# Thirty-two unused floats between the work tiles and the tiles of high parts, in a two-layer mLSTM and retention trunk

## The chip, the cores and the metric

The kernel runs on one core of one Trainium2 chip. The metric is the device time of one execution in microseconds. A core has a matrix engine (PE), three engines for elementwise work (VectorE or DVE, ScalarE or ACT, GpSimd or POOL), a queue engine that issues most transfers (SyncE or SP), and an on-chip memory, SBUF, of 128 partitions. A tile takes the same stretch of bytes in every partition, and that stretch starts at one address. The whole case is about those addresses.

## What is computed

Each of two layers takes x (1024 positions by 1024 features, float32) through

    h = RMSNorm(x) * (1 + scale) + shift          # scale, shift, gate from a conditioning vector
    p = h @ W_in                                  # queries, keys, values, gates for 8 heads of 256
    y_m = sigmoid(o) * LN(mLSTM(conv(q), conv(k), v)) * silu(z)   # heads 0 to 3, chunkwise
    y_r = LN(retention(rot(q), rot(k), v)) * silu(z)              # heads 4 to 7, chunkwise
    x = x + gate * (concat(y_m, y_r) @ W_out)

and a last RMSNorm follows. Nearly all arithmetic is in the two projections, W_in (1024 by 9224) and W_out (2048 by 1024).

## The kernel before

**Split products.** Float32 factors are split in two: a high part, rounded to the matrix engine's float32r, and a low part, the rest. `mm3` (L176 to L179) makes one product of three matmuls: high by high (L177), high by low (L178), low by high (L179). The first argument is the one held in the array (the weights of that matmul, loaded anew for each of the three); the second is streamed past it.

**Where the split tiles live.** The forms of h, the split outputs of the heads and the split keys of the state update lie in the pool `big`, whose 59 tiles of 512 floats are called `b`. A weight block arrives by a transfer in a tile `R`. `high` (L402) copies it on ACT to a tile `wH`, and `low` (L407 to L410) subtracts on DVE or POOL and writes the low part to another `R` tile. So a split weight block is one `wH` and one `R`. In the attention, `q` and `kc` hold high and low part of a chunk's queries and keys in one tile each; `cH`, `cL` hold the split state, `sH`, `sL` the split scores, `ring0` and `ring1` the values.

**Which tile is streamed and which is held.** In the paired products for q, k, z and o (`pair_product`, L758), in the first layer's output projection (`out_units`, L1278) and in the first blocks of a layer, the forms `b` are streamed (512 columns) and `wH`, `R` are held. In the products for v (`vpair_product`, L793; 256 columns) and in the last layer's output projection (512 columns) it is the other way round: `wH`, `R`, `wH` are streamed and `b` is held. The scores stream `q` past `kc` (`diagonal`, L1037, and `mm3`).

**Order.** The order of PE's instructions is the one written. The other engines' order is made by a planner that simulates the program, with priorities and a few places where the written order is kept. A generator clock (`launch`, `tick`) decides when side work is written.

**Addresses.** Three pools lie one after the other in SBUF: `cst`, `big`, `wrk`. In `wrk`, a tag's slots lie together, and tags follow in the order of their first use: `rows`, `R` (12 slots), `wgr`, `q` (2), `acc` (12), `wH` (5), then `sm1`, `cH`, `cL`, `COL`, `kc` and the small tiles, `dm`, `nd`, `sH`, `sL`, `cf`, `zt`. Slots are rounded up to 32 bytes. `b`, `R` and `q` have slots that are whole multiples of 256 bytes, so all of them start at one remainder modulo 256: 64. A slot of `acc` has 516 floats, 2064 bytes, rounded up to 2080. Twelve of them make 24960 bytes, which is 97 times 256 and 128 more. So everything after `acc` lies 128 bytes off: `wH` starts at remainder 192. In `cH` and `cL` the remainders are 0 and 32, in `kc` 64, in `sH` and `sL` 128, in `ring0` and `ring1` 64 and 96.

Of the kernel before, what the change touches and what calls it, by code (L numbers as in the profile page):

```python
# [11 lines left out]
F32 = mybir.dt.float32  # L12
# [7 lines left out]
P = 128  # L20
# [67 lines left out]
def tile_hybrid_trunk(ctx, tc, x, xt, c, positions, w_ada, b_ada, norm_g, w_in, w_blk, w_val, conv_w, conv_b,  # L88
# [9 lines left out]
    wrk = ctx.enter_context(tc.tile_pool(name="wrk", bufs=2))  # L98
# [6 lines left out]
    def nm(s):  # L105
        uid[0] += 1
        return f"{s}_{uid[0]}"

    def bt(dt=F32, n=512):
        return big.tile([P, n], dt, tag="b", name=nm("b"))  # L110

    def wt(tag, n, bufs, dt=F32):
        t = wrk.tile([P, 516 if tag == "acc" else n], dt, tag=tag, bufs=bufs, name=nm(tag))
        return t[:, 0:n] if tag == "acc" else t

    def ps_a():
# [101 lines left out]
    def load_ada_rows(l):  # L218
        rows = wt("rows", P, 2)
        Q.dma_start(rows[0:8, :], norm_g[l].rearrange("(r c) -> r c", c=P))  # L220
        Q.dma_start(rows[8:32, :], b_ada[l].rearrange("(r c) -> r c", c=P))
        return rows

    def load_head_rows(l):
        rows = wt("rows", P, 2)
        Q.dma_start(rows[0:16, :], conv_b[l].rearrange("(r c) -> r c", c=P))
        Q.dma_start(rows[16:80, :], conv_w[l].rearrange("t (r c) -> (t r) c", c=P))
        Q.dma_start(rows[80:88, :], gn_m[l].rearrange("(r c) -> r c", c=P))
        Q.dma_start(rows[88:96, :], gn_r[l].rearrange("(r c) -> r c", c=P))
        bg = cst.tile([P, 1], F32, tag=f"bg{l}", name=f"bg{l}")  # L230
        Q.dma_start(bg[0:4, :], b_fgate[l].unsqueeze(1))
        Q.dma_start(bg[32:36, :], b_igate[l].unsqueeze(1))
        return rows, bg
# [37 lines left out]
    def finish_gsh(l, k, n, psh, psc):  # L271
        cl = cols[l][0]
        V.tensor_tensor(gsh[l][:, 1, k:k + n], psh, cl[:, 104 + k:104 + k + n], ALU.add)
        t1 = wt("sm1", 4, 2)[:, 0:n]
        V.scalar_tensor_tensor(t1, psc, 1.0, cl[:, 112 + k:112 + k + n], ALU.add, ALU.add)
        V.tensor_tensor(gsh[l][:, 0, k:k + n], t1, cl[:, k:k + n], ALU.mult)
# [1194 lines left out]
    for l in range(DEPTH):  # L1471
# [23 lines left out]
        if l == 0:  # L1495
# [10 lines left out]
            for step in script.split():  # L1506
# [4 lines left out]
                if what in "SQ":  # L1511
                    half, tt, cc = arg
                    o, xi, acc = wt("acc", 512, NACC), xts[half][tt][cc], xss[half][:, tt, cc:cc + 1]
# [208 lines left out]
```

## Time and profile before

| | |
|---|---|
| median of three runs | 2225.32 us (2223.43 to 2238.9) |
| the profiled execution | 2226.27 us, of which the span of its instructions 2224.6 us |
| PE, matmuls | 2137.0 us busy, 96% of the span |
| PE, weight loads (beside the matmuls) | 1820.5 us, 82% |
| DVE | 1776.2 us, 80% |
| ACT | 1146.9 us, 52% |
| POOL | 945.0 us, 42% |

A matmul row's duration runs from its start to a modelled end, and matmuls overlap: the next one starts well before the end of the last. So rows of equal shape are compared with one another, and the rate of a stretch is read from the starts in the order of time. In a row such as `px<-b,wH` the first name after the arrow is the streamed tile and the second the held one.

### The profile page before, as it was taken

How to read it: one execution, taken by the hardware profiler on the slowest of the kernel's cores; microseconds unless marked ns; L12 is line 12 of the kernel's file. 1: busy time of each engine (PE TensorE's matmuls, PEld its weight loads, DVE VectorE, ACT ScalarE, POOL GpSimd, SP SyncE). 2: the span in 40 equal slices, each digit the busy share in tenths (PEclk: the TensorE clock that was granted, in tenths of full speed). 3: DMA queues.
4: the chain of work that ended last, by engine and by line, in shares of the span. 5: the costliest groups of instructions: out<-in, count | busy, mean ns of one | idle time of the engine just before them, and what ended most of it. 6: DMA issues, size and time to landing. Idle time of an engine off the chain costs nothing.

```text
span 2224.6 us, 35050 instructions
## 1 busy us (share of the span) xinstructions
PE 2137.0 (96%) x11489; PEld 1820.5 (82%) x11489; DVE 1776.2 (80%) x3139; ACT 1146.9 (52%) x2151; POOL 945.0 (42%) x820
## 2 busy tenths in 40 slices
PE   6899999999999999999999999999999899999998
PEld 5688888878988878888778788888988887888887
DVE  6898897989989988874639697888897798978563
ACT  7545335445556655653544434454555565655442
POOL 1443244444454454424466334444544444352313
PEclk9999999999999999999999999999999999999999
DMA  8268678787787767686632866877877676677874
GB/s 287 60 186 229 196 216 255 211 237 211 214 240 180 202 178 208 192 269 221 208 107 68 250 190 191 230 200 206 234 194 191 177 217 197 171 199 250 222 250 118
DMA packets 452836, 448.44 MB, mean 202 GB/s; under 512 B 191314, under 2 KB 310042, under 8 KB 452652
## 3 DMA queue, kind: packets, MB, share of 16 engines
q1 hardware_dynamic: 432924, 410.27, 59.8%
q0 software_dynamic: 19584, 35.66, 10.7%
q8 instruction: 90, 1.47, 0.3%
q14 instruction: 94, 0.77, 0.1%
q10 hardware_dynamic: 144, 0.26, 0.0%
HBM read 322.76 MB, written 123.31 MB: 201 GB/s over the span
## 4 chain that ended last, share of the span: by engine, by line
PE 54%; DVE 23%; DMA 11%; issue 6%; ACT 3%; POOL 2%; SPq 1%; DVEq 0%; POOLq 0%; ACTq 0%
PE px L177 7%; PE px L178 7%; PE px L179 7%; PE pz L179 6%; PE pz L178 6%; PE pz L177 6%; PE pa L179 4%; PE pa L177 4%; PE pa L178 4%; DVE acc L890 3%; DMA acc<-kfr 3%; DVE R L409 2%; DVE acc L635 2%; DMA R<-in_w_val_dram 2%; PE pa L1131 1%
## 5 line engine op out<-in xcount | busy, mean ns | idle before, releaser
L404 ACT CAST wH<-R 128x512 fp32r<-128x512 f32 x616 | 378.8, 619 | 469.2 <-PE px L178 137.6
L409 POOL TENSOR_TENSOR R<-R,wH 128x512 fp32r<-128x512 f32 x276 | 395.0, 1437 | 483.2 <-ACT wH L404 314.9
L177 PE MATMUL px<-b,wH 128*128 128x512 f32 x912 | 362.4, 397 | 2.9 <-ACT acc L776 1.8
L179 PE MATMUL px<-b,R 128*128 128x512 f32 x912 | 363.0, 398 | 0.0
L178 PE MATMUL px<-b,wH 128*128 128x512 f32 x912 | 361.9, 397 | 0.0
L409 DVE TENSOR_TENSOR R<-R,wH 128x512 fp32r<-128x512 f32 x340 | 262.8, 776 | 92.1 <-ACT wH L404 88.9
L178 PE MATMUL pz<-b,wH 128*128 128x512 f32 x704 | 279.0, 396 | 1.2 <-DVE b L1267 1.2
L179 PE MATMUL pz<-b,R 128*128 128x512 f32 x704 | 279.8, 397 | 0.0
L177 PE MATMUL pz<-b,wH 128*128 128x512 f32 x704 | 278.4, 396 | 0.0
L177 PEld LDWEIGHTS px<-b,wH 128*128 128x128 f32 x912 | 172.9, 190 | 42.0 <-ACT acc L776 3.5
L179 PEld LDWEIGHTS px<-b,R 128*128 128x128 f32 x912 | 172.3, 189 | 40.8
L178 PEld LDWEIGHTS px<-b,wH 128*128 128x128 f32 x912 | 172.8, 189 | 38.7
L177 PE MATMUL px<-wH,b 128*128 128x256 f32 (+1 forms) x576 | 176.9, 307 | 25.8 <-DVE acc L833 13.2
L178 PE MATMUL px<-R,b 128*128 128x256 f32 (+1 forms) x576 | 174.2, 302 | 7.4 <-DVE R L409 7.4
L179 PE MATMUL px<-wH,b 128*128 128x256 f32 (+1 forms) x576 | 174.9, 304 | 0.0
L710 POOL DMA_DIRECT2D R<-in_w_blk_dram x104 | 92.4, 889 | 173.0 <-DMA R<-in_w_blk_dram 68.4
L178 PEld LDWEIGHTS pz<-b,wH 128*128 128x128 f32 x704 | 132.7, 188 | 31.7 <-DVE b L1267 2.0
L179 PEld LDWEIGHTS pz<-b,R 128*128 128x128 f32 x704 | 132.6, 188 | 31.2
L177 PEld LDWEIGHTS pz<-b,wH 128*128 128x128 f32 x704 | 132.9, 189 | 28.5 <-issue 0.2
L177 PEld LDWEIGHTS px<-wH,b 128*128 128x128 f32 x576 | 114.5, 199 | 30.5 <-issue 11.9
L878 POOL TENSOR_TENSOR kc<-acc,kc 128x512 fp32r<-128x512 f32 x64 | 89.5, 1398 | 115.9 <-ACT kc L877 110.8
L177 PE MATMUL pz<-wH,b 128*128 128x256 f32 (+1 forms) x448 | 134.3, 300 | 0.4 <-DVE acc L786 0.2
(343 smaller groups left out, 5308.7 us busy)
## 6 DMA issues: line engine op xcount, KB each, us to landing
R<-in_w_blk_dram SPq DMA_DIRECT2D x276, 256.0 KB
vdr<-acc SPq DMA_DIRECT2D x128, 256.0 KB
ring<-vdr SPq DMA_DIRECT2D x64, 512.0 KB
R<-in_w_out_dram SPq DMA_DIRECT2D x128, 256.0 KB
R<-in_w_blk_dram POOLq DMA_DIRECT2D x104, 256.0 KB, 4.6
R<-in_w_val_dram SPq DMA_DIRECT2D x80, 256.0 KB
gdr<-acc SPq DMA_DIRECT2D x64, 256.0 KB
acc<-in_w_ada_dram SPq DMA_DIRECT2D x64, 256.0 KB
```

The costliest lines, as they stand in the source:

```text
L177: PE.matmul(o, lt[0], rt[0], start=start, stop=False, skip_group_check=more)
L178: PE.matmul(o, lt[0], rt[1], start=False, stop=False, skip_group_check=more)
L179: PE.matmul(o, lt[1], rt[0], start=False, stop=stop, skip_group_check=more)
L404: A.copy(h, r)
L409: eng.tensor_tensor(lo, r, f(h), ALU.subtract)
L635: V.tensor_tensor(t, f(pair[0]), f(pair[1]), ALU.add)
L710: G.dma_start(raw[n], src, accum_op=ALU.add)
L878: eng.tensor_tensor(dst[1], src, f(dst[0]), ALU.subtract)
L890: V.scalar_tensor_tensor(acc[:, e:], pt[:, o + e - d:o + HALF - d], wcol, acc[:, e:], ALU.mult, ALU.add)
L1131: PE.matmul(pi[:, 0:W], piece(qs[j], i, dt, tt * P, P), state[part][:, dt, 0:W], start=part + dt + i == 0, stop=ml and part + dt == 2)
```

## The change

The first time that a tile of the tag `acc` is taken, a further tile of 32 floats (128 bytes) a partition is taken from the same pool, in one slot under the tag `apart`. No instruction reads or writes it. It lies behind `acc` and ahead of `wH`, so that all tags after `acc` move up by 128 bytes.

```diff
+    apart = []
+
     def wt(tag, n, bufs, dt=F32):
         t = wrk.tile([P, 516 if tag == "acc" else n], dt, tag=tag, bufs=bufs, name=nm(tag))
+        if tag == "acc" and not apart:
+            apart.append(wrk.tile([P, 32], F32, tag="apart", bufs=1, name="apart"))
         return t[:, 0:n] if tag == "acc" else t
```

| tile | remainder modulo 256 before | after |
|---|---|---|
| `b`, `R`, `q` | 64 | 64 |
| `wH` | 192 | 64 |
| `kc` | 64 | 192 |
| `cH`, `cL` | 0, 32 | 128, 160 |
| `sH`, `sL` | 128 | 0 |
| `ring0`, `ring1`, `acc` | unchanged | unchanged |

## Prediction

> **What bounds the kernel now.** I read the head of the page first, then the busy shares, then the clock, then the chain of work that ended last.
>
> ```profile
> span 2224.6 us, 35050 instructions
> PE 2137.0 (96%) x11489; PEld 1820.5 (82%) x11489; DVE 1776.2 (80%) x3139; ACT 1146.9 (52%) x2151; POOL 945.0 (42%) x820
> PEclk9999999999999999999999999999999999999999
> PE 54%; DVE 23%; DMA 11%; issue 6%; ACT 3%; POOL 2%; SPq 1%; DVEq 0%; POOLq 0%; ACTq 0%
> ```
>
> PE has a matmul in flight in 96% of the span, at a clock that is granted nearly in full. The chain is on PE for only 54% of the span; the rest of it runs over DVE, transfers and others, while PE is mostly busy beside them. So a gain or a loss per matmul should reach the end with a share between 0.54 and 0.96 of its sum. I take the middle, 0.75.
>
> The change adds no instruction and takes none away. It moves addresses, so its cost can only lie in how long single instructions take. First the elementwise engines, by the costliest groups and the groups by line:
>
> ```profile
> L404 ACT CAST wH<-R 128x512 fp32r<-128x512 f32 x616 | 378.8, 619 | 469.2 <-PE px L178 137.6
> L877 ACT CAST q<-acc 128x512 fp32r<-128x512 f32 x64 | 39.7, 620 | 42.3 <-DMA acc<-qdr 42.1
> L409 POOL TENSOR_TENSOR R<-R,wH 128x512 fp32r<-128x512 f32 x276 | 395.0, 1437 | 483.2 <-ACT wH L404 314.9
> L878 POOL TENSOR_TENSOR q<-acc,q 128x512 fp32r<-128x512 f32 x64 | 92.8, 1450 | 72.3 <-ACT q L877 70.6 <-PE pa L179 1.7
> ```
>
> ACT's copy from remainder 64 to 192 (`wH<-R`) takes 619 ns, and its copy from `acc`, which lies at eight different remainders, to 64 takes 620. POOL's subtraction takes 1437 ns over tiles 128 bytes apart and 1450 over a mixture. No address shows there, so I cost ACT, POOL, and DVE by analogy, at nothing.
>
> Then the matmuls, in the groups by line with shapes kept apart. These carry the counts and, in the two output projections, undisturbed durations:
>
> ```profile
> L178 PE MATMUL px<-b,wH 128*128 128x512 f32 x912 | 361.9, 397 | 0.0
> L178 PE MATMUL pz<-b,wH 128*128 128x512 f32 x704 | 279.0, 396 | 1.2 <-DVE b L1267 1.2
> L177 PE MATMUL pa<-b,wH 128*128 128x512 f32 x128 | 50.3, 393 | 0.0
> L178 PE MATMUL pa<-b,wH 128*128 128x512 f32 x128 | 50.6, 395 | 0.0
> L179 PE MATMUL pa<-b,R 128*128 128x512 f32 x128 | 50.9, 397 | 0.0
> L177 PE MATMUL pa<-wH,b 128*128 128x512 f32 x128 | 50.3, 393 | 0.0
> L178 PE MATMUL pa<-R,b 128*128 128x512 f32 x128 | 49.7, 388 | 0.0
> L179 PE MATMUL pa<-wH,b 128*128 128x512 f32 x128 | 50.1, 391 | 0.0
> L178 PE MATMUL px<-R,b 128*128 128x512 f32 x64 | 24.8, 388 | 0.0
> L178 PE MATMUL pz<-R,b 128*128 128x512 f32 x64 | 24.9, 388 | 0.0
> ```
>
> Equal shapes do not take equal times. In the last layer's output projection the matmul that streams `R` (64) while weights from `b` (64) are loaded takes 388 ns; those that stream `wH` (192) past the same `b` take 393 and 391. The starts in the order of time give the rates, first where `b` is streamed, then where `wH` and `R` are:
>
> ```profile
> 999.96 0.39 PE L177 MATMUL pa<-b,wH 128*128 128x512 f32 x1
> ...
> 1002.76 0.39 PE L177 MATMUL pa<-b,wH 128*128 128x512 f32 x1
> ```
>
> ```profile
> 2069.89 0.39 PE L177 MATMUL pz<-wH,b 128*128 128x512 f32 x1
> ...
> 2072.64 0.39 PE L177 MATMUL pz<-wH,b 128*128 128x512 f32 x1
> ```
>
> Twelve matmuls lie between each pair: 2.80 us is 233.3 ns each, 2.75 us is 229.2. The same work runs 1.8% faster with the roles exchanged. The matmul rate does depend on where the tiles lie, or on which is streamed.
>
> **The change part by part.** Call two tiles "in step" when their remainders are equal, "apart" when they differ by 128. While one matmul streams, the weights of the next are loaded; I compare the streamed tile with the one loaded then.
>
> (a) `b` streamed. There are 912 + 704 + 128 = 1744 triples. In L177 and L179 the weights loaded meanwhile come from `wH` (the second L178 load, and the next block), apart now and in step afterwards. In L178 they come from `R`, in step before and after. What being in step is worth with `b` streamed is seen where the second layer begins, in a stretch (1146 to 1181 us) where three weight blocks take turns and one has its high part in `q` (64):
>
> ```profile
> L1490 PE MATMUL pz<-b,R 128*128 128x512 f32 x12 | 4.8, 397 | 0.0
> L1490 PE MATMUL px<-b,R 128*128 128x512 f32 x12 | 4.7, 395 | 0.0
> L1493 PE MATMUL pz<-b,wH 128*128 128x512 f32 x12 | 4.8, 400 | 0.0
> L1493 PE MATMUL px<-b,wH 128*128 128x512 f32 x12 | 4.7, 393 | 0.0
> ```
>
> The `pz` matmuls load `wH` next (apart), the `px` ones load `q` next (in step): 397 against 395, and 400 against 393. I take the smaller difference, 2 ns, because the larger also changes the matmul that follows. Two matmuls of each triple gain it: 4 ns by 1744 is 7.0 us. The ends: if all three came to the best row seen, 388, the gain would be 5 + 7 + 9 = 21 ns, 36.6 us; if all came to the worst, 400, the loss would be 7 + 5 + 3 = 15 ns, 26.2 us. Within the triple now, L178 (in step) is no faster than the mean of the other two, 395; that is why I stay near the small end.
>
> (b) The last layer's output projection, 64 + 64 + 128 = 256 triples. L177 and L179 stream `wH` and come in step with `b`. At 388 for all three, 5 + 3 = 8 ns by 256 is 2.0 us. The other end is that all take the rows of (a), 393, 395, 397: 0 + 7 + 6 = 13 ns lost, 3.3 us.
>
> (c) The products for v stream `wH`, `R`, `wH` with 256 columns, and (d) the scores stream `q` past `kc`:
>
> ```profile
> L177 PE MATMUL px<-wH,b 128*128 128x256 f32 x512 | 151.8, 296 | 25.8 <-DVE acc L833 13.2 <-ACT acc L826 5.6 <-DVE acc L890 5.4
> L177 PE MATMUL pz<-wH,b 128*128 128x256 f32 x384 | 109.2, 284 | 0.4 <-DVE acc L786 0.2 <-DVE acc L890 0.2
> L178 PE MATMUL pz<-R,b 128*128 128x256 f32 x384 | 107.9, 281 | 0.0
> L179 PE MATMUL pz<-wH,b 128*128 128x256 f32 x384 | 108.7, 283 | 0.0
> L1041 PE MATMUL pa<-q,kc 128*128 128x256 f32 x384 | 56.1, 282 | 0.0
> L178 PE MATMUL pa<-q,kc 128*128 128x256 f32 x64 | 18.0, 281 | 0.0
> ```
>
> For (c) there are 512 + 384 = 896 triples. In step at 281, L177 gains 3 ns and L179 gains 2: 5 ns by 896 is 4.5 us. The other end is none, since `q` past `kc`, in step throughout, averages 282, hardly under the mean of the three rows, 282.7.
>
> For (d) the change works backwards: `kc` goes to 192 and falls apart from `q`. That is 384 + 3 x 64 = 576 matmuls; from 282 to 284, the row of `wH` past `b`, is 2 ns each, 1.2 us lost. So the split tiles don't all come to one remainder. `cH` keeps its distance of 64 bytes from `q` (0 becomes 128, on the other side of 64), and `sH`, against `ring0`, likewise (128 becomes 0). I cost both at nothing.
>
> The sum is 7.0 + 2.0 + 4.5 - 1.2 = 12.3 us of PE's time, by 0.75 some 9 us of the span. The cover that takes the rest is the work of DVE and the transfers beside PE. If matmuls get faster, the weight tiles are wanted earlier, and the longest waits of the wait list are next to be late:
>
> ```profile
> POOL R L409 <- ACT wH L404: 314.9, 100, 23.8
> DVE R L409 <- ACT wH L404: 88.9, 46, 16.7
> ```
>
> POOL and DVE wait there for ACT's copy to `wH`, and ACT waits for PE to give `wH` back. A faster PE returns it earlier, so this ring speeds up with PE.
>
> The span is 2224.6 us, the profiled execution 2226.27, the median 2225.32. The forecast for the median is 2225.3 - 9.2 = 2216 us.
>
> A rule speaks against all of this. The Trainium skill, SBUF — State Buffer, section "Who interferes with whom", gives PE two independent read ports, one for the moving operand and one for the weight load, and says that PE never waits on anyone. By that rule every term above is nothing, and the time stays 2225 us. The rows 388 and 393, equal in shape and neighbours in time, speak against it here, though not against its being right about what causes them.
>
> **The rivals.** First: nothing changes. The rates repeat so exactly from triple to triple that they look like a settled rhythm, in which one matmul's gain is paid back by the next; L178 at 395 between 393 and 397 fits. It would also be so if the tile were not placed where it is said, or the slots not packed. Time: 2225, give or take 3.
>
> Second: what makes the last projection fast is that its streamed tile alternates between 192 and 64, while `b` always lies at 64. Then (a) gains nothing, since `b` doesn't alternate after the change either; (c) and (d) hardly move, since `q` past `kc` shows 282 without alternating; and (b) loses 13 ns a triple, 3.3 us, on a path that is PE's alone. Time: 2228 or 2229, slower. It decides when the `pa<-R,b` row leaves 388 for 393 or above. Against it: 400 against 393 in the layer start, where nothing alternates.
>
> Third: in step is bad when all three matmuls have it. The triple of (a) settles at the worst row, 400: 26.2 us, with 3.3 from (b) and 1.2 from (d) 30.7 us, by 0.75 some 23: 2248. For it: a settled rhythm has to settle somewhere, and 400 occurs. Against it: every direct pair of rows puts in step ahead.
>
> Fourth: the triple of (a) settles at the best row: 36.6 + 2.0 + 4.5 - 1.2 = 41.9 us, by 0.54 to 0.96 a gain of 23 to 40: 2185 to 2203.
>
> **How the numbers follow.** The forecast (gains of 3 to 18 us) gets 0.39, nothing 0.32, the alternation 0.14, the bad rhythm 0.07, the best rhythm 0.08. No change and a change of up to 1% (22 us) can hardly be told apart by a measurement of this kernel, whose three runs spread over 15 us. Faster than 2203 is most of the fourth case and a tail of the forecast: 0.10. Slower than 2247.6 is half of the third, and a little for what no row shows: 0.05. The rest, 0.85, is within 1%. For the range I leave out about half of the third and half of the fourth case: 2197 to 2240. Cases of a loss are in it, but the likeliest case alone has 2207 to 2222.
>
> **What would show it.** The count of instructions and the order on each engine stay, or the argument is void. `pa<-wH,b` L177 and L179 at 388 show (b) right; L178 above 391 shows the alternation. `pa<-b,wH` L177 and `pa<-b,R` L179 should lose 2 ns or more, and twelve starts should span less than 2.80 us. `pa<-q,kc` should rise to 284. ACT's copy stays at 619. The prediction is wrong if twelve starts span 2.80 us again, or more, or if they span 2.72 or less: then the distance between two tiles at the start of a matmul isn't what sets the rhythm.

## The result

| | before | after |
|---|---|---|
| median of 14 runs each | 2225.64 us | 2218.6 us (2208.86 to 2223.85) |
| ratio of after to before | | 0.9958, 95% interval 0.994 to 0.9976 |
| span of the profiled execution | 2224.6 us | 2219.1 us |

The interval leaves out 1, so the kernel became faster by 0.24 to 0.6%, 9.3 us by the ratio (7.0 by the two medians). Two more measurements of the same kernel, told below, gave 0.9951 and 0.9952, 10.9 and 10.7 us. The forecast was 2216 us, a gain of 9.2 us; the time lies in the range and in the likeliest case. That the number came out is no proof that its terms did: the size of one, the sign of another and the share that reaches the end were wrong.

The line numbers after the change are higher by four. The order of the instructions on each engine is the same, one by one, with the same operands and the same waits. The head of the page after, then its clock, the chain of work that ended last, and the two costliest groups of ACT and POOL:

```profile
span 2219.1 us, 35050 instructions
PE 2116.1 (95%) x11489; PEld 1827.4 (82%) x11489; DVE 1785.4 (80%) x3139; ACT 1141.9 (51%) x2151; POOL 949.2 (43%) x820
PEclk9999999999999999999999999999999999999999
PE 17%; DVE 5%; DMA 2%; issue 1%; POOL 1%; SPq 0%; ACT 0%; POOLq 0%; DVEq 0%; ACTq 0%
L408 ACT CAST wH<-R 128x512 fp32r<-128x512 f32 x616 | 377.6, 617 | 413.0 <-PE px L182 102.0
L413 POOL TENSOR_TENSOR R<-R,wH 128x512 fp32r<-128x512 f32 x276 | 393.9, 1437 | 457.3 <-ACT wH L408 290.0
```

PE's busy time fell by 20.9 us, the span by 5.5. The copy on ACT (617 ns after 619) and the subtraction on POOL (1437 both times) show nothing of the addresses. The shares of the chain add up to only 26% here, so the chain was followed over a part of the span and isn't compared with the one of before.

The groups by line after, shapes kept apart: the last columns are the busy time in us, the mean of one in ns, and the idle time ahead of them.

```profile
L181 PE MATMUL pa<-b,wH 128*128 128x512 f32 x128 | 49.8, 389 | 0.0
L182 PE MATMUL pa<-b,wH 128*128 128x512 f32 x128 | 49.8, 389 | 0.0
L183 PE MATMUL pa<-b,R 128*128 128x512 f32 x128 | 49.8, 389 | 0.0
L181 PE MATMUL pa<-wH,b 128*128 128x512 f32 x128 | 49.8, 389 | 0.0
L182 PE MATMUL pa<-R,b 128*128 128x512 f32 x128 | 49.8, 389 | 0.0
L182 PE MATMUL pz<-R,b 128*128 128x256 f32 x384 | 109.3, 285 | 0.0
L1045 PE MATMUL pa<-q,kc 128*128 128x256 f32 x384 | 56.7, 284 | 0.1
```

The matmuls with 512 columns in these undisturbed rows have come to one value, 389, whichever of the two tiles is streamed; before they took 388 to 397. Those with 256 columns went the other way, `pz<-R,b` from 281 to 285 and `pa<-q,kc` from 282 to 284. The starts in the order of time give the rates: `b` streamed, then the beginning of the second layer, then `wH` and `R` streamed.

```profile
999.99 0.39 PE L181 MATMUL pa<-b,wH 128*128 128x512 f32 x1
...
1002.71 0.39 PE L181 MATMUL pa<-b,wH 128*128 128x512 f32 x1
...
1146.62 0.39 PE L1493 MATMUL pz<-b,wH 128*128 128x512 f32 x1
...
1148.66 0.39 PE L1493 MATMUL pz<-b,wH 128*128 128x512 f32 x1
...
2065.18 0.39 PE L181 MATMUL px<-wH,b 128*128 128x512 f32 x1
...
2067.91 0.39 PE L181 MATMUL px<-wH,b 128*128 128x512 f32 x1
```

Twelve starts take 2.72 us where they took 2.80, and 2.73 where they took 2.75; the nine of the layer's beginning take 2.04 us. All three are 227 ns a start. So one matmul of 512 columns costs 226.7 ns now, against 233.3 with `b` streamed and 229.2 the other way round.

**What this is worth on PE.** I took the distances between the starts of all 11,489 matmuls of each profiled execution, and of every kernel told of below. The mean of a triple that no wait interrupts, in ns:

| triple | times | before | after |
|---|---|---|---|
| `b` streamed, 512 columns (a) | 1744 | 699.6 | 683.0 |
| `wH`, `R`, `wH` streamed, 512 columns (b) | 256 | 686.8 | 680.0 |
| `wH`, `R`, `wH` streamed, 256 columns (c) | 896 | 358.4 | 359.5 |
| `q` past `kc`, 256 columns (d) | 576 matmuls, taken on 64 triples of them | 355.4 | 361.1 |

In (a), 1272 of the 1688 triples seen take 680 to the nanosecond; the rest bring the mean to 683. The change is 16.6 x 1744 = 29 us from (a), 1.7 from (b), minus 1.0 from (c), minus 1.1 from (d): 28.6 us. About a third of it, 9 to 11 us, is seen in the time.

**Where the rest went.** The span cut at the same matmuls in both executions (the stages are named by the time before). "Streaming" is what the starts of undisturbed matmuls take; "waits" is what longer distances exceed that by; "clock" is the excess in the short stretches where the granted clock is near half.

| stage, us | streaming before, after | waits before, after | clock before, after | stage before, after |
|---|---|---|---|---|
| 0 to 120 | 100.0, 99.9 | 11.1, 9.8 | 8.9, 9.2 | 120.1, 118.9 |
| 120 to 900 | 740.3, 730.7 | 24.0, 29.4 | 15.6, 20.2 | 780.0, 780.3 |
| 900 to 1146 | 239.5, 234.0 | 6.4, 7.3 | 0, 0 | 245.9, 241.3 |
| 1146 to 1300 | 142.7, 140.6 | 3.1, 4.4 | 8.2, 7.6 | 154.0, 152.6 |
| 1300 to 2000 | 666.7, 657.5 | 17.0, 33.2 | 16.3, 13.1 | 700.0, 703.7 |
| 2000 to the end | 213.9, 211.4 | 0, 0 | 0, 0 | 213.9, 211.4 |

Streaming is shorter by 29.0 us. Where PE hardly waits, in the first layer's output projection (900 to 1146) and behind 2000, 7.1 of 8.0 us arrive. In the two long stages of attention, convolutions and normalization, 18.8 us are won in streaming, and PE's waits grow by 21.6. In the two further profiles of this kernel the waits over the whole span grew by 13 and 14 us instead of 23; the clock's part differs from one execution to the next (its stretches sum to 60.7 us before, and to 70.2, 54.4 and 63.7 in the three profiles after).

Over all executions on record the clock does have a direction, which the two profiles above don't show, since the profiled execution of before (0.987) was one with a low clock. The mean granted clock is 0.9892 in the 64 executions of before that ran beside the experiments, and 0.9863 in the 28 executions of the change. An estimate from these numbers: with the clock at 0.50 in the low stretches, that is some 12 us more of them in an execution, and a matmul of 256 columns takes 214 ns there instead of 120, so some 5 us of the gain may be lost on the clock rather than in waits. What lowers it stays open: in the kernels with less work for DVE, told below, PE is busy for 97 to 98% of the span and the clock is higher, 0.994 and 0.993.

Which waits these are, in the list of PE's waits of before (us in total, times, longest):

```profile
PE px L177 <- ACT acc L776: 1.8, 3, 1.0
PE pa L179 <- DVE b L930: 2.6, 6, 0.6
PE pa L1122 <- ACT sH L1079: 2.5, 3, 1.8
PE pa L1131 <- DVE cL L1105: 2.3, 2, 1.3
```

and the same waits after:

```profile
PE px L181 <- ACT acc L780: 5.4, 4, 2.0
PE pa L183 <- DVE b L934: 4.3, 6, 1.0
PE pa L1126 <- ACT sH L1083: 4.7, 5, 1.4
PE pa L1135 <- DVE cL L1109: 3.8, 3, 1.7
```

No single wait takes the gain. These four, which were there before, became longer by 1.5 to 3.6 us each in total. Two of them end at ACT and two at DVE, so the list alone doesn't say which engine PE follows. Beside them stand the windows of the two long stages (columns: window; its length, then busy us and count of PE, PEld, DVE, ACT, POOL; granted clock, DMA share, GB/s). Before:

```profile
120.00:900.00 780.00, 754.00 (x4272) 654.86 (x4272) 698.52 (x1277) 405.78 (x776) 343.86 (x303) 0.99 0.76 212
1300.00:2000.00 700.00, 680.12 (x3855) 592.56 (x3854) 587.76 (x1065) 375.32 (x731) 319.61 (x292) 0.99 0.73 201
```

and after:

```profile
120.00:900.00 780.00, 748.62 (x4267) 658.78 (x4266) 697.97 (x1280) 404.25 (x775) 341.15 (x303) 0.98 0.76 212
1300.00:2000.00 700.00, 671.00 (x3846) 591.64 (x3845) 590.60 (x1059) 372.80 (x732) 324.26 (x292) 0.98 0.73 199
```

PE is busy for 5 and 9 us less and starts no more matmuls in the same time. DVE is busy for 698 of the 780 us and 588 of the 700, the same before and after. That suggests that PE already worked to DVE's pace there; whether it did is tested below.

### The profile page after: what moved, and what is told of

It reads as the page before. It is cut to its first block, busy times and chain, and to the rows that moved or that the text cites. A ratio compares the mean times of both kernels' runs of the same rounds, so it can differ in the third digit from the quotient of the medians.

```text
span 2219.1 us, 35050 instructions
## 1 busy us (share of the span) xinstructions
PE 2116.1 (95%) x11489; PEld 1827.4 (82%) x11489; DVE 1785.4 (80%) x3139; ACT 1141.9 (51%) x2151; POOL 949.2 (43%) x820
## 5 line engine op out<-in xcount | busy, mean ns | idle before, releaser
L413 POOL TENSOR_TENSOR R<-R,wH 128x512 fp32r<-128x512 f32 x276 | 393.9, 1437 | 457.3 <-ACT wH L408 290.0
L181 PE MATMUL px<-b,wH 128*128 128x512 f32 x912 | 361.1, 396 | 7.6 <-ACT acc L780 5.4
L182 PE MATMUL pz<-b,wH 128*128 128x512 f32 x704 | 275.5, 391 | 1.6 <-DVE b L1271 1.6
L181 PE MATMUL pz<-b,wH 128*128 128x512 f32 x704 | 276.0, 392 | 0.0
L183 PE MATMUL pz<-b,R 128*128 128x512 f32 x704 | 275.1, 391 | 0.0
L182 PEld LDWEIGHTS px<-b,wH 128*128 128x128 f32 x912 | 173.6, 190 | 33.2
L181 PEld LDWEIGHTS px<-wH,b 128*128 128x128 f32 x576 | 115.5, 201 | 31.5 <-issue 13.1
```

The costliest lines, as they stand in the source:

```text
L181: PE.matmul(o, lt[0], rt[0], start=start, stop=False, skip_group_check=more)
L182: PE.matmul(o, lt[0], rt[1], start=False, stop=False, skip_group_check=more)
L183: PE.matmul(o, lt[1], rt[0], start=False, stop=stop, skip_group_check=more)
L413: eng.tensor_tensor(lo, r, f(h), ALU.subtract)
```

## The experiments

The theory behind the forecast, A: the distance modulo 256 between the streamed tile and the tile of the weights loaded meanwhile sets the rate, in step or out of it. (`b` and `R` start at 64 in every kernel here; of the three tiles only `wH` moves.) The rivals: B, only the old place 192 of `wH` is bad, and any other gives the same; C, what moved behind `wH` (the tiles of the attention) makes the gain. On where the gain went: D, PE follows DVE in the long stages.

**Other distances.** The number of unused floats sets the place of `wH`: 8, 16 and 24 floats instead of 32 put it 96, 64 and 32 bytes from `b`.

```diff
-            apart.append(wrk.tile([P, 32], F32, tag="apart", bufs=1, name="apart"))
+            apart.append(wrk.tile([P, 8], F32, tag="apart", bufs=1, name="apart"))
```

> Eight floats instead of thirty-two: wH starts at remainder 224, 96 bytes from b and R on the short way round; kc at 96, 32 bytes from q. Theory A (the distance between the streamed tile and the weights that are loaded meanwhile sets the rhythm): twelve starts in the first layer's output projection span neither the 2.80 us of before nor the 2.72 us of the change, but some value of their own between 2.69 and 2.86; the three rows of a triple are unequal. Theory B (only remainder 192 of wH was bad, any other is good): 2.72 us and 389 ns in all three rows. Time by A: 2219 to 2228 us; by B: as the change, 2217 to 2220.

```diff
-            apart.append(wrk.tile([P, 32], F32, tag="apart", bufs=1, name="apart"))
+            apart.append(wrk.tile([P, 16], F32, tag="apart", bufs=1, name="apart"))
```

> Sixteen floats: wH starts at remainder 0, 64 bytes from b and R; kc at 128, 64 bytes from q. Theory A: twelve starts span a value of its own, not 2.72 us, rows of a triple unequal. Theory B: 2.72 us and 389 ns in all three rows. If 64 bytes were the period of the effect, this kernel too would show 2.72 us, but then the 128 bytes of before would have shown it as well. Time by A: 2219 to 2228 us; by B: 2217 to 2220.

```diff
-            apart.append(wrk.tile([P, 32], F32, tag="apart", bufs=1, name="apart"))
+            apart.append(wrk.tile([P, 24], F32, tag="apart", bufs=1, name="apart"))
```

> Twenty-four floats: wH starts at remainder 32, 32 bytes short of b and R; kc at 160. Theory A: again a rhythm of its own, rows of a triple unequal, twelve starts not at 2.72 us. Theory B: 2.72 us and 389 ns in all three rows. Whatever the rhythm, if the other engines and transfers set the pace outside the output projections, the time moves by a third or less of the sum of what the matmuls gain or lose against before.

Measured, with the mean of a triple in ns counted as above:

| floats | `wH` at | from `b` | (a) | (b) | (c) | median, us | ratio to before |
|---|---|---|---|---|---|---|---|
| 0 (before) | 192 | 128 | 699.6 | 686.8 | 358.4 | 2222.73 | 1 |
| 8 | 224 | 96 | 694.6 | 696.7 | 354.4 | 2222.29 | 1.0 (0.9983 to 1.0018) |
| 16 | 0 | 64 | 689.9 | 703.1 | 355.5 | 2220.5 | 0.9991 (0.9975 to 1.0007) |
| 24 | 32 | 32 | 699.6 | 699.9 | 353.5 | 2226.05 | 1.0021 (1.0001 to 1.0042) |
| 32 (after) | 64 | 0 | 683.0 | 680.0 | 359.5 | 2218.6 | 0.9958 (0.994 to 0.9976) |

The groups by line with 8 floats, then 16, then 24:

```profile
L181 PE MATMUL pa<-b,wH 128*128 128x512 f32 x128 | 50.4, 394 | 0.0
L182 PE MATMUL pa<-b,wH 128*128 128x512 f32 x128 | 50.3, 393 | 0.0
L183 PE MATMUL pa<-b,R 128*128 128x512 f32 x128 | 50.2, 392 | 0.0
```

```profile
L181 PE MATMUL pa<-b,wH 128*128 128x512 f32 x128 | 50.3, 393 | 0.0
L182 PE MATMUL pa<-b,wH 128*128 128x512 f32 x128 | 50.0, 391 | 0.0
L183 PE MATMUL pa<-b,R 128*128 128x512 f32 x128 | 49.9, 390 | 0.0
L181 PE MATMUL pa<-wH,b 128*128 128x512 f32 x128 | 50.9, 398 | 0.0
L182 PE MATMUL pa<-R,b 128*128 128x512 f32 x128 | 51.0, 399 | 0.0
```

```profile
L181 PE MATMUL pa<-b,wH 128*128 128x512 f32 x128 | 50.8, 397 | 0.0
L182 PE MATMUL pa<-b,wH 128*128 128x512 f32 x128 | 50.8, 397 | 0.0
L183 PE MATMUL pa<-b,R 128*128 128x512 f32 x128 | 50.3, 393 | 0.0
```

The medians come from different sets of runs (the kernel before had 2225.64 beside the change and 2222.73 beside the other three), so the ratios are what to compare. Only the change leaves 1 on the fast side.

The gain in time is no fixed share of PE's. By the table PE's matmuls win 9.8, 15.3 and 1.0 us with 8, 16 and 24 floats, and the time changed by 0, -2.0 and +4.7 us. The interval at 24 floats, 0.2 to 9.3 us slower, isn't the third or less of PE's sum that was expected there; why that kernel is slower is open.

Theory B falls: at 96, 64 and 32 bytes the rate isn't that of the change, and 32 bytes are as slow as 128. The place of `wH` does set the rate. Whether its distance from `b` and `R` counts, or the place 64 by itself, these kernels can't tell apart, since `b` and `R` never move; a kernel that moves all three together would. The order of the distances isn't simple: with `b` streamed the distances 64, 96, 32 and 128 follow from good to bad; with the roles exchanged it is 128, 96, 32 and 64. Nor is it a sum over single matmuls: in all these kernels the distance of `R` from `b` is nil, and yet `pa<-R,b` takes 399 at 16 floats, where it took 388 before. The three matmuls of a triple share one rhythm. Both roles are at their best in step. They agree there within 3 ns, and also at 32 bytes, where both are near 700. For 256 columns, in step is the slowest place of the five.

**Only `wH`.** Its slots are taken ahead of those of `acc`. So `wH` lies at 64, and all else lies modulo 256 as before.

```diff
+        if tag == "acc" and not apart:
+            apart.append(wrk.tile([P, 512], F32R, tag="wH", bufs=NW, name="apart"))
         t = wrk.tile([P, 516 if tag == "acc" else n], dt, tag=tag, bufs=bufs, name=nm(tag))
```

> The wH tiles stand ahead of acc, with no unused floats: wH is at remainder 64, and everything behind acc (kc 64, cH 0, cL 32, sH 128) is where it was before. Theory A (the gain is wH in step with b and R): twelve starts span 2.72 us, 389 ns in all rows of both output projections, q past kc back at 282 ns from 284; time 2216 to 2219 us, as the change or up to 1.5 us below. Rival C (the gain came from the attention's tiles, which the change moved as well): 2.80 us for twelve starts, and the time of before.

Measured: 2216.23 us, 0.9982 (0.9968 to 0.9995). Groups by line of this kernel:

```profile
L181 PE MATMUL pa<-b,wH 128*128 128x512 f32 x128 | 49.8, 389 | 0.0
L1045 PE MATMUL pa<-q,kc 128*128 128x256 f32 x384 | 56.4, 283 | 0.0
```

The triples (a) and (b) take 682.7 and 680.2, as with the change. So `wH` alone makes the rate, and rival C falls there. The time seemed to give back less than the change's, so both were run again:

> The change itself once more, beside a run of before and of kc_only on one chip: 0.994 to 0.998 of before. It also tells whether the gap between it (0.9958) and wh_only (0.9982) is more than the chip's spread.

> wH in step by its place ahead of acc, all else where it was; on one chip with the change (after_third) and wh_kc. If the other engines take most of what PE gains, this and the change lie within 3 us of each other, both 0.994 to 0.999 of before; a gap above 4 us would mean that the attention's tiles do matter to the time.

> The change once more beside the other two: 0.994 to 0.998 of before.

Measured: the change 0.9951 (0.9931 to 0.9972) and 0.9952 (0.9933 to 0.9971), medians 2211.91 and 2212.52 us; `wH` alone 0.9957 (0.9939 to 0.9974), median 2214.79. All these intervals overlap. What the first measurement of `wH` alone suggested, that the attention's tiles bring a part of the gain, isn't borne out.

**Only what lies behind `wH`.** The 32 floats are placed between `wH` and `cH`, so that `wH` stays at 192 and `cH`, `cL`, `kc`, `sH` and `sL` move as in the change.

```diff
-        if tag == "acc" and not apart:
+        if tag == "wH" and not apart:
             apart.append(wrk.tile([P, 32], F32, tag="apart", bufs=1, name="apart"))
```

> The thirty-two floats stand behind wH and ahead of cH: wH stays at 192, while kc, cH, cL, sH and all behind are 128 bytes on, as in the change. Theory A (only wH in step pays): twelve starts 2.80 us, q past kc at 284 ns, time 0.999 to 1.002 of before. Rival C (the attention's tiles bring the gain): 2.80 us, but the time of the change, 0.996.

Measured: 2221.1 us, 0.9997 (0.998 to 1.0015). Groups by line of this kernel:

```profile
L181 PE MATMUL pa<-b,wH 128*128 128x512 f32 x128 | 50.3, 393 | 0.0
L183 PE MATMUL pa<-b,R 128*128 128x512 f32 x128 | 50.9, 397 | 0.0
L1045 PE MATMUL pa<-q,kc 128*128 128x256 f32 x384 | 56.0, 281 | 0.1
```

Rival C falls from this side as well: the rows are those of before, and so is the time. But `pa<-q,kc` doesn't go to 284. With `kc` at 192 it takes 281 here and 284 in the change, and with `kc` at 64 it takes 282 before and 283 with `wH` alone. The distance of `kc` from `q` isn't what decides that row.

**Where the gain went.** To see whether PE's waits are DVE's, DVE is given less to do: the loop over three taps of the convolution and two of three operations of the rotation are left out, first without and then with the 32 floats.

```diff
-        for d in range(1, 4):
-            wcol = cl[:, 24 + 16 * (3 - d) + ct:25 + 16 * (3 - d) + ct]
-            e = 0 if half else d
-            V.scalar_tensor_tensor(acc[:, e:], pt[:, o + e - d:o + HALF - d], wcol, acc[:, e:], ALU.mult, ALU.add)
...
-                s, a = wt("acc", 512, NACC), wt("acc", 512, NACC)
-                V.tensor_tensor(a, n1, two[half], ALU.mult)
-                V.tensor_tensor(s, p0, one[half], ALU.mult)
-                V.tensor_tensor(s, s, a, op)
+                s = wt("acc", 512, NACC)
+                V.tensor_tensor(s, p0 if m == 0 else n1, one[half], ALU.mult)
```

> The kernel before with less work on VectorE: the convolution's three earlier taps and, in the rotation, two of the three operations a half are left out (some 300 instructions, about 230 us by the rows of before), so the outputs are those of other formulas. No unused floats. The base for light1; expected 2170 to 2215 us, twelve starts at 2.80 us.

> light0 with the thirty-two unused floats, the same program otherwise. Absorption (VectorE and what hangs on it set the pace where the gain is lost): with VectorE relieved, more of the 38 us that PE's matmuls gain gets through, 15 to 30 us below light0. Rival (the gain is lost on PE itself, in half-clock windows and in settling after each wait, whatever VectorE does): 5 to 11 us below light0, as in the full kernels.

Measured: 2174.65 us without the floats, 0.9791 (0.9772 to 0.9809), and 2152.62 us with them, 0.9697 (0.9681 to 0.9713): 22.0 us between the two. The busy shares and the window of 120 to 900 us without the floats:

```profile
PE 2120.3 (98%) x11489; PEld 1811.7 (83%) x11489; DVE 1558.4 (72%) x2819; ACT 1146.6 (53%) x2151; POOL 917.5 (42%) x820
```

```profile
120.00:900.00 780.00, 768.84 (x4377) 669.98 (x4376) 603.96 (x1150) 418.50 (x803) 342.91 (x318) 0.99 0.76 217
```

and with them:

```profile
PE 2092.5 (97%) x11489; PEld 1812.5 (84%) x11489; DVE 1553.4 (72%) x2819; ACT 1144.1 (53%) x2151; POOL 918.1 (43%) x820
```

```profile
120.00:900.00 780.00, 765.61 (x4397) 676.13 (x4396) 606.51 (x1158) 419.32 (x808) 341.91 (x318) 0.99 0.77 219
```

The triples take 699.6 and 683.0, 686.8 and 680.1, as in the full kernels, so PE wins the same 29 us. With DVE at 604 of the 780 us instead of 698, 22.0 of them arrive, three quarters, and PE's waits over the span grow by 6 us (33.6 to 39.3) instead of 13 to 23. So twice as much of the same gain reaches the end when DVE has room: theory D stands for a part of the loss. It isn't the whole account of every stretch: between 120 and 900 us the lightened pair, too, is only 3.5 us apart in the two profiles, since its waits grow by 1.2 us but the stretches at half clock by 5.7. What was lightened is DVE as a whole; which of its operations PE follows was not tried. The two lightened kernels have one and the same order on every engine, but ACT's and POOL's order in them isn't that of the full kernels, so the pair is to be compared within itself. The 38 us named in its expectation is 28.6 by the count above.

**One step further.** `wH` ahead of `acc`, and 16 floats behind `acc`, which put `kc` 64 bytes from `q`. With 16 floats in the series above, `pa<-q,kc` had been at 279.

```diff
+        if tag == "acc" and not apart:
+            apart.append(wrk.tile([P, 512], F32R, tag="wH", bufs=NW, name="apart"))
         t = wrk.tile([P, 516 if tag == "acc" else n], dt, tag=tag, bufs=bufs, name=nm(tag))
+        if tag == "acc" and len(apart) == 1:
+            apart.append(wrk.tile([P, 16], F32, tag="apart", bufs=1, name="apart2"))
```

> wh_only with sixteen unused floats behind acc, so that kc starts at 128, 64 bytes from q, the distance at which s16 had its fastest scores (279 ns a row against 282 to 284): twelve starts 2.72 us, q past kc 279 to 280 ns. 576 matmuls by 4 ns are 2.3 us of PE's time against the change; by a fifth to a half of that the time is 0.5 to 1 us below wh_only, too little to be told from it. If the distance of kc to q were what counts for the time, 3 us or more.

Measured: 2213.38 us, 0.9956 (0.9938 to 0.9975). Groups by line of this kernel:

```profile
L183 PE MATMUL pa<-b,wH 128*128 128x512 f32 x128 | 49.9, 389 | 0.0
L1047 PE MATMUL pa<-q,kc 128*128 128x256 f32 x384 | 55.9, 282 | 0.0
```

The row of the scores is at 282, not at 279 or 280, so that expectation failed too. The time is that of the change and of `wH` alone. Of the kernels tried none beats the change.

## Why the prediction was right, and which of its steps were wrong

- **That only addresses move, and that the elementwise engines don't feel them:** right. The order is the same one by one, and the rows of ACT and POOL stand at 617 and 1437 ns.
- **(a), `b` streamed, "4 ns by 1744 is 7.0 us":** the direction was right, the size wrong by four times. The triple lost 16.6 ns, and 20 where it has settled. Two things failed in that step. It took its difference from two pairs of rows of the second layer's beginning and left out others of the same window that don't fit, such as this one, which loads `wH` next (apart) and is as fast as any:

```profile
L1490 PE MATMUL pa<-b,R 128*128 128x512 f32 x12 | 4.7, 392 | 0.0
```

  So not every pair of rows put in step ahead, as the prediction said. In the same window after the change every row of this sequence is at 389, those that were in step already too:

```profile
L1494 PE MATMUL pa<-b,R 128*128 128x512 f32 x10 | 3.9, 389 | 0.0
L1497 PE MATMUL pz<-b,wH 128*128 128x512 f32 x10 | 3.9, 389 | 0.0
```

  And it left L178 at 395, because its own two tiles keep their distance. That row went to 389 with the others. In the first rival the prediction saw that the triple settles in one rhythm, but its sum counted matmul by matmul.
- **(b), the last projection, "5 + 3 = 8 ns":** 6.8 by the starts, 2.0 us predicted and 1.7 found. The row `pa<-R,b` went from 388 to 389 and did not leave for 393, so the second rival, the alternation, is out.
- **(c), the products for v, "a gain of 4.5 us":** wrong in sign. In step costs 1.1 ns a triple, 1.0 us. The step carried over to 256 columns what holds for 512. In the series of distances 256 columns are slowest in step.
- **(d), the scores, 1.2 us lost:** 284 came as written, and 1.1 us. The reason was not right: with only `kc` moved the row stays at 281. What sets it is open.
- **The tiles costed at nothing:** moving `cH`, `cL`, `sH`, `sL` and `kc` together moved the time to 0.9997 (0.998 to 1.0015). Nothing is seen of it.
- **The sum of 12.3 us by 0.75:** the sum was 28.6, and the share that passes 0.33 to 0.38 (9.3 and 10.9 us). That the two errors cancel is luck. The share was taken as the middle of the chain's share on PE, 0.54, and PE's busy share, 0.96. Neither says how much slack the other engines have: in the two long stages DVE is busy for 90 and 84% of the time, and PE's waits grew there as its matmuls became faster. Nor does either hold the clock, on which the forecast says nothing. The bounds 0.54 to 0.96 didn't even hold it. In the kernel with less work for DVE, 0.76 of the gain passes.
- **The rivals:** "nothing changes" is out by the interval. The bad rhythm is out. The best rhythm came true in its rates (389 where it had 388), and its 41.9 us of PE's time are nearer to the 28.6 than my 12.3; its time of 2185 to 2203 did not come, because of the share that passes.
- **What would have shown it wrong:** "if they span 2.72 or less: then the distance between two tiles at the start of a matmul isn't what sets the rhythm". They span 2.72. So the prediction's own sign of being wrong came true. What is refuted is the sum over single matmuls: the series shows that the place of `wH` does set the rhythm, but that of the triple as a whole.
- **The rule cited:** the Trainium skill, SBUF — State Buffer, section "Who interferes with whom", says that PE and ACT never wait on anyone. Here up to 20 ns of 700 hang on nothing but the place of one tile. That doesn't show which part waits for which; no run here separates the weight load from the stream.

## What to carry to other kernels

Where float32r matmuls with a weight load each follow one another, read the start-to-start time of equal shapes, and if it differs between places, compare the remainders of the streamed and the held tile; unused bytes test that with the same program. Multiply what a matmul gains by what passes in its stage: here all of it behind 2000 us, where PE never waits, and a third over the whole kernel, with DVE busy for 84 to 90% of the long stages. A forecast that comes out should still be checked term by term: here two errors of factor two and more made one right number.

## What the runs showed that I had not expected

In step, the two lengths of matmul differ by the time of their columns alone. The starts come 226.7 ns apart with 512 columns and 120 with 256 (360 a triple): the 256 columns between them cost 106.7 ns, and 13.3 ns are over in both. Two lengths alone can always be split in this way, so it needs a second look. A stretch of the timeline of before, in which the granted clock is 0.50 and products for v run, lets one look at the excess; the first line is its window, in which the third number from the end is the clock:

```profile
1368.80:1370.50 1.70, 1.70 (x10) 1.70 (x9) 1.70 (x3) 1.70 (x4) 1.70 (x2) 0.50 0.34 111
```

```profile
1368.79 0.41 PE L177 MATMUL px<-wH,b 128*128 128x256 f32 x1
...
1370.50 0.41 PE L179 MATMUL px<-wH,b 128*128 128x256 f32 x1
```

Eight starts in 1.71 us are 213.8 ns for 256 columns. Twice 106.7 is 213.4, so at half clock nothing is left of the excess, though the tiles were out of step.

The roles differ at some distances and hardly at others: 699.6 and 686.8 at a distance of 128, 689.9 and 703.1 at 64, but 699.6 and 699.9 at 32, and 683.0 and 680.0 in step.

The tiles `R` and `b` on one side and `wH` on the other lie 256 bytes apart modulo 512 after the change, and act as in step. So the period is no longer than 256 bytes, as far as this one case shows.

A gain on PE of 1.3% of the span moved the time by 0.4 to 0.5%, with PE still busy for 95% of the span. That share says that matmuls are in flight, not that they set the end.
